# A row sum over 64 MB: groups of 16 rows on one load queue, VectorE for the bulk, and a last group in falling pieces

## The chip, the cores and the metric

The kernel runs on one core of one Trainium2 chip. The metric is the device time of one execution in microseconds (us). All times below are medians of several executions unless a single profiled one is named. A profiled execution has a *span*, from its first to its last instruction; the measured time of the same execution is about 1.8 us longer. Comparisons use runs called fast. On one core, a run is called slow only when it is over 1.5% above the fastest run of the same kernel.

## The reference

```python
batch, seq, dim = 32, 512, 1024
x = np.random.randn(batch, seq, dim).astype(np.float32)      # 67.1 MB

def reference(x):
    return np.sum(x, axis=-1).astype(np.float32)              # 16,384 sums
```

Each of 16,384 rows of 1,024 floats becomes one sum. The kernel reads 67.1 MB and writes 0.07 MB, with one addition per element read.

## The kernel before

Rows are cut into 16 tiles. A tile has 128 partitions with 8 consecutive rows each, 32 KB per partition. Even tiles are summed by one VectorE reduce, odd tiles by 8 ScalarE activations that accumulate. The loads of the even tiles, and of all tiles from 12 on, are issued by SyncE, those of the odd tiles up to 11 by ScalarE, so two queues are in use. The last two tiles are loaded in four pieces of two rows each.

```python
P, Q = 128, 8;  W = Q * dim;  ntiles = 16
head_launchers = [nc.sync, nc.scalar] * 6
# pools: input tiles bufs=5, scratch bufs=4, one tile "stage" for all sums
for i in range(ntiles):
    t = inpool.tile([P, W], fp32)
    eng = head_launchers[i] if i < len(head_launchers) else nc.sync
    dst = stage[:, i * Q : (i + 1) * Q]
    if i >= ntiles - 2:                       # the last two tiles
        engs = ["s","v","s","v"] if i == ntiles - 2 else ["v","v","v","v"]
        for s in range(4):                    # four loads of 2 rows
            nc.sync.dma_start(out=t[:, s*2*dim : (s+1)*2*dim], in_=...)
        for s in range(4): ...                # "v": one reduce of 2 rows; "s": two activations
    elif i % 2 == 0:
        eng.dma_start(out=t, in_=x_t[i])
        nc.vector.tensor_reduce(out=dst, in_=t.rearrange("p (q d) -> p q d", q=Q),
                                axis=X, op=add)
    else:
        eng.dma_start(out=t, in_=x_t[i])
        for q in range(Q):
            nc.scalar.activation(out=sc, in_=t[:, q*dim:(q+1)*dim], func=Copy,
                                 accum_out=dst[:, q:q+1])
    # after every second tile: store by GpSimd; the last store by SyncE
```

Of the kernel before, what the change touches and what calls it, by code (L numbers as in the profile page):

```python
# [1 line left out]

# [4 lines left out]


@with_exitstack
def kernel(  # L10
    ctx: ExitStack,
    tc: tile.TileContext,
    x: bass.AP,
    out: bass.AP,
):
    nc = tc.nc
    fp32 = mybir.dt.float32

    batch, seq, dim = x.shape
    rows = batch * seq  # L20
    P = 128
    Q = 8
    W = Q * dim
    ntiles = rows // (P * Q)

    x_t = x.flatten_outer_dims().rearrange("(n p q) d -> n p (q d)", p=P, q=Q, n=ntiles)
    out_v = out.rearrange("b s -> (b s)").rearrange("(n p q) -> p n q", p=P, q=Q, n=ntiles)

    bounds = list(range(2, ntiles - 1, 2)) + [ntiles - 1, ntiles]

    head_launchers = [nc.sync, nc.scalar] * 6

    with (
        tc.tile_pool(name="in", bufs=5) as inpool,
        tc.tile_pool(name="scratch", bufs=4) as spool,
        tc.tile_pool(name="stage", bufs=1) as stpool,
    ):
        stage = stpool.tile([P, ntiles * Q], fp32)

        prev = 0  # L40
        for i in range(ntiles):
            t = inpool.tile([P, W], fp32)
            eng = head_launchers[i] if i < len(head_launchers) else nc.sync
            dst = stage[:, i * Q : (i + 1) * Q]
            if i >= ntiles - 2:
                NSUB = 4
                QS = Q // NSUB
                engs = (
                    ["s", "v", "s", "v"] if i == ntiles - 2 else ["v", "v", "v", "v"]
                )  # L50
                for s in range(NSUB):
                    nc.sync.dma_start(
                        out=t[:, s * QS * dim : (s + 1) * QS * dim],
                        in_=x_t[i][:, s * QS * dim : (s + 1) * QS * dim],
                    )
                for s in range(NSUB):
                    sdst = dst[:, s * QS : (s + 1) * QS]
                    if engs[s] == "v":
                        nc.vector.tensor_reduce(  # L59
                            out=sdst,  # L60
                            in_=t[:, s * QS * dim : (s + 1) * QS * dim].rearrange(
                                "p (q d) -> p q d", q=QS
                            ),
                            axis=mybir.AxisListType.X,
                            op=mybir.AluOpType.add,
                        )
                    else:
                        for q in range(s * QS, (s + 1) * QS):
                            sc = spool.tile([P, dim], fp32)
                            nc.scalar.activation(  # L70
                                out=sc,
                                in_=t[:, q * dim : (q + 1) * dim],
                                func=mybir.ActivationFunctionType.Copy,
                                accum_out=dst[:, q : q + 1],
                            )
            elif i % 2 == 0:
                eng.dma_start(out=t, in_=x_t[i])  # L77
                nc.vector.tensor_reduce(  # L78
                    out=dst,
                    in_=t.rearrange("p (q d) -> p q d", q=Q),  # L80
                    axis=mybir.AxisListType.X,
                    op=mybir.AluOpType.add,
                )
            else:
                eng.dma_start(out=t, in_=x_t[i])  # L85
                for q in range(Q):
                    sc = spool.tile([P, dim], fp32)
                    nc.scalar.activation(  # L88
                        out=sc,
                        in_=t[:, q * dim : (q + 1) * dim],  # L90
                        func=mybir.ActivationFunctionType.Copy,
                        accum_out=dst[:, q : q + 1],
                    )
            if (i + 1) in bounds:
                n0, n1 = prev, i + 1
                prev = i + 1
                src = stage[:, n0 * Q : n1 * Q].rearrange("p (n q) -> p n q", q=Q)
                oeng = nc.sync if n1 == ntiles else nc.gpsimd
                oeng.dma_start(out=out_v[:, n0:n1], in_=src)  # L99


# [1 line left out]
_INS = ['x']  # L103
_OUTS = [((32, 512), 'float32')]


# [23 lines left out]
```

## Time and profile before

| | before |
|---|---|
| time, median (range) | 165.8 us (165.76 to 165.94) |
| span of the profiled run | 164.1 us |
| VectorE busy, ScalarE busy | 74.5 us, 64.3 us |
| share of loads in the chain of waits | 86% |

From the page of the profile: the busy time of each engine, the chain that ended last by engine, and the two groups of VectorE reduces (line, engine, operation, tiles, shapes, count, then busy time and mean ns of one, then idle time before them and what ended it).

```profile
DVE 74.5 (45%) x13; ACT 64.3 (39%) x121; POOL 5.9 (4%) x12
...
DMA 86%; DVE 7%; ACT 5%; issue 0%; ACTq 0%; SPq 0%
...
L78 DVE TENSOR_REDUCE stage<-t 128x8 f32<-128x8192 f32 x7 | 60.8, 8686 | 71.6 <-DMA t<-in_x_dram 71.6
L59 DVE TENSOR_REDUCE stage<-t 128x2 f32<-128x2048 f32 x6 | 13.7, 2286 | 15.6 <-DMA t<-in_x_dram 15.6
```

Both engines that add (DVE is VectorE, ACT is ScalarE) are idle more than half the time, and what ends their idle time is a load (apart from 1.7 us of ScalarE at the start). So the loads set the kernel's time. A row costs VectorE (8,686 - 2,286) / 6 = 1,067 ns, and a reduce has about 150 ns on top.

The end of the chain of waits of the kernel before, in order of time (start us, us, what):

```profile
99.84 39.72 DMA t<-in_x_dram
139.55 0.02 issue
139.57 19.87 DMA t<-in_x_dram
159.44 0.02 issue
159.47 2.29 DVE stage L59
```

Tile 13 landed at 139.55 us and the last piece at 159.44 us. Then one reduce of two rows takes 2.29 us, and the final store and the end of the program take the other 2.3 us of the span. There are two places to gain: the loads, and the 4.7 us after the last load.

### The profile page before, as it was taken

The numbers are of one execution on the slowest core, as the hardware profiler recorded it, in microseconds if no ns is written. First come the engines' busy times: TensorE is split into PE (matmuls) and PEld (weight loads), VectorE is DVE, ScalarE is ACT, GpSimd is POOL, SyncE is SP. The second block draws the span as 40 slices with busy tenths as digits, with TensorE's granted clock in tenths as the row PEclk, the third lists the DMA queues.
The fourth block names the chain that finished last, engine by engine and source line by source line (L and its number), as shares of the span: only waits on it lengthen the run. The fifth ranks groups of instructions, "written<-read, shape, count | busy, mean of one in ns | idle before, by whom it ended". The sixth has DMA issues, their size and how long they took to land.

```text
span 164.1 us, 241 instructions
## 1 busy us (share of the span) xinstructions
DVE 74.5 (45%) x13; ACT 64.3 (39%) x121; POOL 5.9 (4%) x12
## 2 busy tenths in 40 slices
DVE  0000049600794990039700892595008920055994
ACT  3000049600693000099101980000496006999940
POOL 0000000200001000000100001000001000010110
DMA  7899999998999989999999899999999998999960
GB/s 256 383 479 415 407 479 391 447 449 383 503 391 439 457 384 471 423 407 479 391 441 455 385 471 415 409 479 399 439 447 391 472 417 383 421 423 419 423 243 1
DMA packets 3569, 67.18 MB, mean 409 GB/s; under 512 B 640, under 2 KB 752, under 8 KB 752
## 3 DMA queue, kind: packets, MB, share of 16 engines
q1 hardware_dynamic: 2448, 41.95, 60.1%
q10 hardware_dynamic: 864, 25.17, 35.5%
q0 software_dynamic: 256, 0.06, 0.2%
q14 instruction: 1, 0.01, 0.0%
HBM read 67.11 MB, written 0.07 MB: 409 GB/s over the span
## 4 chain that ended last, share of the span: by engine, by line
DMA 86%; DVE 7%; ACT 5%; issue 0%; ACTq 0%; SPq 0%
DMA t<-in_x_dram 86%; DVE stage L78 5%; ACT sc L88 5%; DVE stage L59 1%; ACTq L85 0%; SPq L77 0%; SPq L85 0%; ACTq L88 0%
## 5 line engine op out<-in xcount | busy, mean ns | idle before, releaser
L88 ACT ACTIVATE sc<-t 128x1024 f32<-128x1024 f32 x56 | 58.3, 1041 | 91.7 <-DMA t<-in_x_dram 91.7
L78 DVE TENSOR_REDUCE stage<-t 128x8 f32<-128x8192 f32 x7 | 60.8, 8686 | 71.6 <-DMA t<-in_x_dram 71.6
L59 DVE TENSOR_REDUCE stage<-t 128x2 f32<-128x2048 f32 x6 | 13.7, 2286 | 15.6 <-DMA t<-in_x_dram 15.6
L99 POOL DMA_DIRECT2D out_dram<-stage x8 | 5.7, 718 | 152.3 <-ACT sc L88 98.8
L88 ACT ACTIVATION_READ_ACCUMULATOR sc<-t 128x1 f32 x56 | 10.4, 186 | 0.0
L70 ACT ACTIVATE sc<-t 128x1024 f32<-128x1024 f32 x4 | 4.2, 1039 | 0.0
L88 ACT ACT_TABLE_LOAD x1 | 1.3, 1283 | 1.7 <-PEq L114 1.7
L70 ACT ACTIVATION_READ_ACCUMULATOR sc<-t 128x1 f32 x4 | 0.7, 185 | 0.0
L114 POOL MEMSET const-float32-0.0<- 128x1 f32 x1 | 0.1, 99 | 0.2 <-issue 0.2
L114 POOL MEMSET const-bfloat16-1.0<- 128x1 bf16 x1 | 0.1, 102 | 0.0
L114 POOL MEMSET const-float32-1.0<- 128x1 f32 x1 | 0.1, 99 | 0.0
L114 POOL MEMSET const-uint8-127<- 128x1 uint8 x1 | 0.1, 99 | 0.0
## 6 DMA issues: line engine op xcount, KB each, us to landing
t<-in_x_dram SPq DMA_DIRECT2D x8, 4096.0 KB, 39.8
t<-in_x_dram ACTq DMA_DIRECT2D x6, 4096.0 KB, 31.0
t<-in_x_dram SPq DMA_DIRECT2D x8, 1024.0 KB, 27.5
out_dram<-stage POOLq DMA_DIRECT2D x7, 8.0 KB, 8.0
out_dram<-stage POOLq DMA_DIRECT2D x1, 4.0 KB, 1.7
out_dram<-stage SPq DMA_DIRECT2D x1, 4.0 KB, 1.4
```

The source lines that it names most:

```text
L59: nc.vector.tensor_reduce(out=sdst, in_=t[:, s * QS * dim : (s + 1) * QS * dim].rearrange("p (q d) -> p q d", q=QS), axis=mybir.AxisListTy ...
L70: nc.scalar.activation(out=sc, in_=t[:, q * dim : (q + 1) * dim], func=mybir.ActivationFunctionType.Copy, accum_out=dst[:, q : q + 1],)
L78: nc.vector.tensor_reduce(out=dst, in_=t.rearrange("p (q d) -> p q d", q=Q), axis=mybir.AxisListType.X, op=mybir.AluOpType.add,)
L88: nc.scalar.activation(out=sc, in_=t[:, q * dim : (q + 1) * dim], func=mybir.ActivationFunctionType.Copy, accum_out=dst[:, q : q + 1],)
L99: oeng.dma_start(out=out_v[:, n0:n1], in_=src)
L114: nc = _bacc.Bacc("TRN2", target_bir_lowering=False, num_devices=1)
```

## The change

The intent: larger loads (16 rows, 64 KB per partition), all issued by SyncE; VectorE alone sums six of the seven large groups, and the two engines share the seventh; the eighth group comes in pieces of 8, 4, 2 and 1 rows, and its very last row in 384, 384 and 256 columns, so that little is left to add after the last landing; the sums of the first groups are stored by GpSimd while loads still run. The diff, cut to its core:

```diff
-    Q = 8
-    x_t = x.flatten_outer_dims().rearrange("(n p q) d -> n p (q d)", p=P, q=Q, n=ntiles)
-    head_launchers = [nc.sync, nc.scalar] * 6
-        tc.tile_pool(name="in", bufs=5)  ...  scratch bufs=4
+    BIG = 16
+    x_g = x.flatten_outer_dims().rearrange("(g p j) d -> g p j d", p=P, j=BIG)
+    nbig = J // BIG - 1                       # 7
+    tail = [(8, 4), (4, 2), (2, 1)]           # (rows, of them ScalarE's)
+        tc.tile_pool(name="in", bufs=3)  ...  scratch bufs=1
...
+        def rows_of(t, a, n, j, n_act):
+            nv = n - n_act
+            block = t[:, a * dim : (a + n) * dim].rearrange("p (n d) -> p n d", d=dim)
+            nc.sync.dma_start(out=block, in_=rows_from(j, n))
+            if nv:
+                vec(sums[:, j : j + nv], block[:, :nv, :])
+            for q in range(nv, n):
+                act(sums[:, j + q : j + q + 1], block[:, q, :], dim)
...
+        for i in range(nbig):
+            t = inpool.tile([P, BIG * dim + 2], fp32)
+            rows_of(t, 0, BIG, i * BIG, BIG // 2 if i == nbig - 1 else 0)
+            if i % 3 == 2:
+                store(nc.gpsimd, i - 2, i + 1)
+        store(nc.gpsimd, nbig - 1, nbig)
+        t = inpool.tile([P, BIG * dim + 2], fp32)
+        for n, n_act in tail:
+            rows_of(t, a, n, nbig * BIG + a, n_act);  a += n
+        rows_of(t, a, 1, nbig * BIG + a, 1);  a += 1
+        last = t[:, a * dim :]
+        cuts = [0, 384, 768, dim]
+        for c0, c1 in zip(cuts, cuts[1:]):
+            nc.sync.dma_start(out=last[:, c0:c1], in_=rows_from(j, 1)[:, 0, c0:c1])
+        # partial sums of columns 0-383 and 384-767 go to the two cells behind the row,
+        # so the last reduce adds 256 columns and the two partial sums: 258 elements
+        store(nc.sync, nbig, nbig + 1)
```

In what follows, a *descriptor* is one contiguous piece of a load, here one partition's rows, moved by one of the 16 DMA engines. The traces show it as a packet: each load has 128, 8 per engine.

More of the change, by code (lines that the diff above doesn't have):

```diff
@@ L17 @@
     fp32 = mybir.dt.float32
+    P = 128
     batch, seq, dim = x.shape
     rows = batch * seq
-    P = 128
-    Q = 8
-    W = Q * dim
-    ntiles = rows // (P * Q)
-    x_t = x.flatten_outer_dims().rearrange("(n p q) d -> n p (q d)", p=P, q=Q, n=ntiles)
-    out_v = out.rearrange("b s -> (b s)").rearrange("(n p q) -> p n q", p=P, q=Q, n=ntiles)
-    bounds = list(range(2, ntiles - 1, 2)) + [ntiles - 1, ntiles]
-    head_launchers = [nc.sync, nc.scalar] * 6
+    J = rows // P
+    BIG = 16
+    x_g = x.flatten_outer_dims().rearrange("(g p j) d -> g p j d", p=P, j=BIG)
@@ L33, with rows_from @@
+    out_v = out.rearrange("b s -> (b s)").rearrange("(g p j) -> p g j", p=P, j=BIG)
+    def rows_from(j, n):
+        return x_g[j // BIG, :, j % BIG : j % BIG + n, :]
+    nbig = J // BIG - 1
+    tail = [(8, 4), (4, 2), (2, 1)]
     with (
-        tc.tile_pool(name="in", bufs=5) as inpool,
-        tc.tile_pool(name="scratch", bufs=4) as spool,
+        tc.tile_pool(name="in", bufs=3) as inpool,
+        tc.tile_pool(name="scratch", bufs=1) as spool,
         tc.tile_pool(name="stage", bufs=1) as stpool,
@@ L37 @@
     ):
-        stage = stpool.tile([P, ntiles * Q], fp32)
-        prev = 0
-        for i in range(ntiles):
-            t = inpool.tile([P, W], fp32)
-            eng = head_launchers[i] if i < len(head_launchers) else nc.sync
-            dst = stage[:, i * Q : (i + 1) * Q]
-            if i >= ntiles - 2:
-                NSUB = 4
-                QS = Q // NSUB
-                engs = (
-                    ["s", "v", "s", "v"] if i == ntiles - 2 else ["v", "v", "v", "v"]
-                )
-                for s in range(NSUB):
-                    nc.sync.dma_start(
-                        out=t[:, s * QS * dim : (s + 1) * QS * dim],
-                        in_=x_t[i][:, s * QS * dim : (s + 1) * QS * dim],
-                    )
-                for s in range(NSUB):
-                    sdst = dst[:, s * QS : (s + 1) * QS]
-                    if engs[s] == "v":
-                        nc.vector.tensor_reduce(
-                            out=sdst,
-                            in_=t[:, s * QS * dim : (s + 1) * QS * dim].rearrange(
-                                "p (q d) -> p q d", q=QS
-                            ),
-                            axis=mybir.AxisListType.X,
-                            op=mybir.AluOpType.add,
-                        )
-                    else:
-                        for q in range(s * QS, (s + 1) * QS):
-                            sc = spool.tile([P, dim], fp32)
-                            nc.scalar.activation(
-                                out=sc,
-                                in_=t[:, q * dim : (q + 1) * dim],
-                                func=mybir.ActivationFunctionType.Copy,
-                                accum_out=dst[:, q : q + 1],
-                            )
-            elif i % 2 == 0:
-                eng.dma_start(out=t, in_=x_t[i])
-                nc.vector.tensor_reduce(
-                    out=dst,
-                    in_=t.rearrange("p (q d) -> p q d", q=Q),
-                    axis=mybir.AxisListType.X,
-                    op=mybir.AluOpType.add,
-                )
-            else:
-                eng.dma_start(out=t, in_=x_t[i])
-                for q in range(Q):
-                    sc = spool.tile([P, dim], fp32)
-                    nc.scalar.activation(
-                        out=sc,
-                        in_=t[:, q * dim : (q + 1) * dim],
-                        func=mybir.ActivationFunctionType.Copy,
-                        accum_out=dst[:, q : q + 1],
-                    )
-            if (i + 1) in bounds:
-                n0, n1 = prev, i + 1
-                prev = i + 1
-                src = stage[:, n0 * Q : n1 * Q].rearrange("p (n q) -> p n q", q=Q)
-                oeng = nc.sync if n1 == ntiles else nc.gpsimd
-                oeng.dma_start(out=out_v[:, n0:n1], in_=src)
@@ new lines, with vec, act @@
+        sums = stpool.tile([P, J], fp32)
+        scratch = spool.tile([P, dim], fp32)
+        def vec(dst, src):
+            nc.vector.tensor_reduce(
+                out=dst, in_=src, axis=mybir.AxisListType.X, op=mybir.AluOpType.add
+            )
+        def act(dst, src, n):
+            nc.scalar.activation(
+                out=scratch[:, :n],
+                in_=src,
+                func=mybir.ActivationFunctionType.Copy,
+                accum_out=dst,
+            )
+        def rows_of(t, a, n, j, n_act):
[6 more added lines that the diff above has]
+                act(sums[:, j + q : j + q + 1], block[:, q, :], dim)
@@ new lines, in store @@
+        def store(eng, g0, g1):
+            eng.dma_start(
+                out=out_v[:, g0:g1],
+                in_=sums[:, g0 * BIG : g1 * BIG].rearrange("p (g j) -> p g j", j=BIG),
+            )
+        for i in range(nbig):
[5 more added lines that the diff above has]
+        t = inpool.tile([P, BIG * dim + 2], fp32)
@@ new lines @@
+        a = 0
+        for n, n_act in tail:
+            rows_of(t, a, n, nbig * BIG + a, n_act)
+            a += n
+        rows_of(t, a, 1, nbig * BIG + a, 1)
+        a += 1
+        j = nbig * BIG + a
+        last = t[:, a * dim :]
+        cuts = [0, 384, 768, dim]
+        for c0, c1 in zip(cuts, cuts[1:]):
+            nc.sync.dma_start(out=last[:, c0:c1], in_=rows_from(j, 1)[:, 0, c0:c1])
+        for i, (c0, c1) in enumerate(zip(cuts, cuts[1:])):
+            if c1 < dim:
+                vec(last[:, dim + i : dim + i + 1], last[:, c0:c1])
+            else:
+                vec(sums[:, j : j + 1], last[:, c0 : dim + i])
```

## The prediction

> **What bounds the kernel now.** The loads. In the chain of waits the loads hold 86% of the 164.1 us span; VectorE is busy 45% and ScalarE 39% (busy table). Tiles 0 and 1 land at 22.6 us and tile 13 at 139.55 us (idle before the first reduces, and the chain): 50.3 MB in 117 us, 430 GB/s. The last two tiles, cut into 8 KB rows per partition, land from 139.55 to 159.44 us: 8.39 MB at 422 GB/s. After the last landing come one 2,286 ns VectorE reduce (2 rows), a 0.35 us issue, and about 2 us of store and end; the unprofiled time is 1.7 us over the span.
>
> **What the change does, costed.**
>
> 1. Bulk work moves from half VectorE, half ScalarE to VectorE alone. The 8-row reduce takes 8,686 ns, the 2-row one 2,286 ns: about 1,067 ns a row and 150 ns fixed. A 16-row group then costs about 17.2 us (estimate) against 19.5 us between group landings. VectorE keeps pace; with three buffers, load k+3 is issued about 2 us before load k+1 lands, with load k+2 queued. So the move is off the critical path, gain zero.
>
> 2. Descriptor size. From the two rates, one engine takes about 1,218 ns for 32 KB and 311 ns for 8 KB: about 8 ns fixed plus 27.1 B/ns (estimate; the Trainium skill, "DMA: Bandwidth & Descriptors", section "Where 436 GB/s comes from", gives a fabric ceiling of 435 GB/s). Descriptors per engine fall from 176 to 112: about 0.5 us. If the 16 rows stayed 4 KB descriptors, the fit gives 411 GB/s, a loss of several us.
>
> 3. One queue instead of two: nothing. The skill (same page, "Issuing engines are not separate DMA queues") says that issuing from several engines saves only sequencer time; an issue here takes 0.33 us.
>
> 4. The end. The last piece is 256 columns. Its reduce over 258 elements is estimated at 0.42 us, against 2.29 us now. Pieces arrive about 0.3 to 0.45 us apart, and the two 384-column reduces (about 0.55 us each) lag slightly, so VectorE ends some 0.7 us after the last landing: about 1.6 us gained. ScalarE's last row (1.04 + 0.19 us) lands 1.2 us before the end and just fits. The final store stays.
>
> 5. Fewer GpSimd stores (8 become 3): these queues moved 0.06 MB, 0.2% of the DMA; gain 0.1 us or none.
>
> **Sum.** 165.8 - 1.6 (end) - 0.5 (descriptors) = 163.7 us; 8 in 10 between 162.8 and 164.8. Faster by over 2% (under 162.5): 0.07; within 2%: 0.90; slower by over 2%: 0.03.
>
> **What would show it.** Group landings about 19.5 us apart, about 431 GB/s between them. VectorE about 75% busy, idle before each group's reduce for about 2 us. Load packets fall as counted. The last load lands at about 158.9 us. After it VectorE works 0.6 to 0.8 us, and the chain ends with that, the SyncE store and about 2 us.
>
> **What would make it wrong.** Rows not merged into one descriptor (slower, 168 to 170). A slower read pattern from the 64 KB spacing of partitions. Late issue of load k+3, if the wait for VectorE leaves too little queued. Small transfers at the end completing later than their bytes explain; or ScalarE's last row or a GpSimd store ending last. On the good side: costs of descriptors or of two queues greater than fitted.

## The result, and the profile after

The changed kernel takes 163.84 us (163.67 to 164.03) against 165.8 us. The ratio is 0.9879, with a 95% interval of 0.9865 to 0.9893. A ratio here is the mean time of one kernel's fast runs over that of the other's in the same rounds, so it is not quite the ratio of the medians. The gain of 2.0 us is clear of the noise.

From the page of the profile after: busy times, the load queue (packets, MB, share of 16 engines), the chain by engine, and the issue of the very last piece (KB, us to landing).

```profile
DVE 121.4 (75%) x13; ACT 19.7 (12%) x33; POOL 2.4 (1%) x7
...
q1 hardware_dynamic: 2160, 67.12, 96.6%
...
DMA 74%; DVE 22%; SPq 1%; issue 0%; DVEq 0%
...
t<-in_x_dram SPq DMA_DIRECT2D x1, 128.0 KB, 38.4
```

The timeline of VectorE after (start us, us, engine, line, operation, tiles, count; in brackets the idle time before it and what ended it; the line at 153.70 merges a two-row and a one-row reduce):

```profile
22.78 17.22 DVE L44 TENSOR_REDUCE sums<-t 128x16 f32<-128x16384 f32 x1 [22.78 <-DMA t<-in_x_dram]
42.11 17.22 DVE L44 TENSOR_REDUCE sums<-t 128x16 f32<-128x16384 f32 x1 [2.11 <-DMA t<-in_x_dram]
...
138.94 8.69 DVE L44 TENSOR_REDUCE sums<-t 128x8 f32<-128x8192 f32 x1 [2.15 <-DMA t<-in_x_dram]
148.68 4.42 DVE L44 TENSOR_REDUCE sums<-t 128x4 f32<-128x4096 f32 x1 [1.05 <-DMA t<-in_x_dram]
153.70 3.62 DVE L44 TENSOR_REDUCE sums<-t 128x2 f32<-128x2048 f32 x2 [0.59 <-DMA t<-in_x_dram]
158.00 1.01 DVE L44 TENSOR_REDUCE t<-t 128x1 f32<-128x384 f32 x2 [0.69 <-DMA t<-in_x_dram]
159.05 0.42 DVE L44 TENSOR_REDUCE sums<-t 128x1 f32<-128x258 f32 x1
```

Each large reduce starts when its group lands, after 2.1 us of waiting: VectorE has 2.1 us to spare per group. From the first landing to the seventh (22.78 to 138.94) six groups take 116.16 us; the kernel before needed 116.95 us for the same bytes (22.6 to 139.55). The changed kernel's second profile, of the next section, has 116.43 us, so such a figure moves by 0.3 us from run to run. The last piece lands at about 158.7 us: it was issued at 120.3 us and took 38.4 us. VectorE ends at 159.47 us, 0.8 us later, where it was 2.3 us before. So the last landing moved forward by some 0.7 us in this pair of profiles, and the time after it shrank by 1.5 us.

### The profile page after: what moved, and what is told of

Its sections match the earlier page's. It is cut to its first block, busy times and chain, and to the rows that moved or that the text cites. A ratio compares the mean times of both kernels' runs of the same rounds, so it can differ in the third digit from the quotient of the medians.

```text
span 161.9 us, 124 instructions
## 1 busy us (share of the span) xinstructions
DVE 121.4 (75%) x13; ACT 19.7 (12%) x33; POOL 2.4 (1%) x7
## 3 DMA queue, kind: packets, MB, share of 16 engines
q1 hardware_dynamic: 2160, 67.12, 96.6%
## 4 chain that ended last, share of the span: by engine, by line
DMA 74%; DVE 22%; SPq 1%; issue 0%; DVEq 0%
DMA t<-in_x_dram 74%; DVE sums L44 22%; SPq L59 1%; DVE t L44 1%; DVEq L44 0%
## 5 line engine op out<-in xcount | busy, mean ns | idle before, releaser
L44 DVE TENSOR_REDUCE sums<-t 128x16 f32<-128x16384 f32 (+5 forms) x11 | 120.4, 10941 | 37.4 <-DMA t<-in_x_dram 37.3
L49 ACT ACTIVATE scratch<-t 128x1024 f32<-128x1024 f32 x16 | 16.9, 1057 | 138.2 <-DMA t<-in_x_dram 137.8
L66 POOL DMA_DIRECT2D out_dram<-sums x3 | 2.2, 733 | 146.6 <-DVE sums L44 135.8
L49 ACT ACTIVATION_READ_ACCUMULATOR scratch<-t 128x1 f32 x16 | 3.0, 186 | 0.0
L44 DVE TENSOR_REDUCE t<-t 128x1 f32<-128x384 f32 x2 | 1.0, 546 | 0.7 <-DMA t<-in_x_dram 0.7
## 6 DMA issues: line engine op xcount, KB each, us to landing
t<-in_x_dram SPq DMA_DIRECT2D x1, 128.0 KB, 38.4
```

What stands on the lines that cost most here:

```text
L44: nc.vector.tensor_reduce(out=dst, in_=src, axis=mybir.AxisListType.X, op=mybir.AluOpType.add)
L49: nc.scalar.activation(out=scratch[:, :n], in_=src, func=mybir.ActivationFunctionType.Copy, accum_out=dst,)
L66: eng.dma_start(out=out_v[:, g0:g1], in_=sums[:, g0 * BIG : g1 * BIG].rearrange("p (g j) -> p g j", j=BIG),)
```

## The experiments

Twelve runs were made, one of them the changed kernel again. Their diffs are cut to the core too, with comments in place of some code. Each call also ran the kernel before on the same chip (medians 165.82 to 165.88 us), and the first of the three calls ran the changed kernel again, as a partner for the others.

> The changed kernel once more, as the partner on this chip for the other three. Both theories: 163.8 us, ratio 0.988 to the kernel before, groups landing 19.36 us apart.

Measured: 163.86 us (163.75 to 163.99), ratio 0.9882. The result repeats.

### Which half gives what: the two ends and the two ways of loading

First the changed kernel with the end of the kernel before:

```diff
-        for n, n_act in tail: rows_of(t, a, n, ...)
-        ... one row, then 384, 384, 256 columns
+        for a in range(0, BIG, 2):
+            rows_of(t, a, 2, nbig * BIG + a, 2 if a in (0, 4) else 0)
```

> The changed kernel with the end of the kernel before: the last 16 rows in eight pieces of two rows, the last four on VectorE. My theory: 1.5 us slower than the changed kernel, 165.3 us, so the loads alone gave 0.4 to 0.5 us. Rival (the bulk gave most): under 0.9 us slower, 164.7 or less.

Measured: 165.33 us, ratio 0.997 (0.9958 to 0.9982). The end is worth 1.5 us on the changed kernel, as expected; the rest of the change is worth 0.5 us.

Then the opposite: the kernel before, of which only the last tile gets falling pieces, all on VectorE.

```diff
+            if i == ntiles - 1:
+                # loads: rows 0-1, 2-3, 4-5, 6, then row 7 in columns 0-383, 384-767, 768-1023
+                # sums: all by VectorE, as in the changed kernel
```

> The kernel before with only its last 8-row tile changed: pieces of 2, 2, 2, 1 rows and of 384, 384 and 256 columns, all on VectorE. My theory: the end alone gives 1.4 to 1.6 us of the 1.9, so 164.3 us; VectorE ends 0.6 to 0.9 us after the last landing instead of 2.3. Rival (most of the gain is from the bulk's loads): under 0.9 us, 164.9 or more.

Measured: 166.03 us, ratio 1.0009 (0.9997 to 1.0022). Nothing was gained. This was a miss, and a useful one. The timeline of VectorE at the end of this kernel, each line from a window around it (the first line merges a two-row and a one-row reduce):

```profile
154.41 2.29 DVE L49 TENSOR_REDUCE stage<-t 128x2 f32<-128x2048 f32 x1 [0.19 <-DMA t<-in_x_dram]
156.91 3.41 DVE L49 TENSOR_REDUCE stage<-t 128x2 f32<-128x2048 f32 x2 [0.22 <-DMA t<-in_x_dram]
160.24 1.00 DVE L49 TENSOR_REDUCE t<-t 128x1 f32<-128x384 f32 x2
161.28 0.42 DVE L49 TENSOR_REDUCE stage<-t 128x1 f32<-128x258 f32 x1
```

The last three lines have no wait for a load. From 156.91 us on, VectorE works without a pause until 161.70 us, and all loads had landed at about 159.6 us (the last was issued at 147.0 and took 12.6). A pair of rows takes VectorE 2.29 us and arrives every 2.49 us, so VectorE is only just ahead, and each further piece adds its fixed cost. Two rows cut into four pieces cost 1.21 + 0.54 + 0.54 + 0.42 = 2.7 us where one reduce took 2.29. These small pieces alone don't shorten the end; the reading to test next is that VectorE must also have less to do there.

So the next kernel took over the whole end: tiles 13 and 14 half on each engine, tile 15 in pieces of 4, 2 and 1 rows shared by both engines, then the three column pieces.

```diff
+            if i >= ntiles - 3:
+                if i < ntiles - 1:
+                    piece(0, Q, Q // 2)          # 4 rows VectorE, 4 rows ScalarE
+                else:
+                    piece(0, 4, 2); piece(4, 2, 1); piece(6, 1, 1)
+                    # row 7 in 384, 384 and 256 columns on VectorE
```

> The kernel before with the whole end of the changed one: tiles 13 and 14 half on each engine, tile 15 in pieces of 4, 2 and 1 rows shared by VectorE and ScalarE, then the last row in 384, 384 and 256 columns. Theory (falling pieces pay only when both engines share them, since a row takes VectorE 1.07 us and arrives every 1.24, and each piece adds a fixed cost): VectorE is done 0.6 to 0.9 us after the last landing, 164.3 us. Rival (the end pays nothing on the 8-row kernel, the gain is tied to the large groups): 165.7 or more.

Measured: 164.12 us (164.06 to 164.25), ratio 0.9898 (0.9884 to 0.9911). Its VectorE at the end:

```profile
156.43 1.22 DVE L49 TENSOR_REDUCE stage<-t 128x1 f32<-128x1024 f32 x1 [0.24 <-DMA t<-in_x_dram]
158.35 1.01 DVE L49 TENSOR_REDUCE t<-t 128x1 f32<-128x384 f32 x2 [0.70 <-DMA t<-in_x_dram]
159.39 0.42 DVE L49 TENSOR_REDUCE stage<-t 128x1 f32<-128x258 f32 x1
```

VectorE waits for the last row again (0.70 us) and is done at 159.81 us. Two more things differ from the kernel that gained nothing: the pieces are of 4, 2 and 1 rows instead of 2, 2, 2 and 1, and tile 14 comes in one load. They were not tested apart from the sharing; the wait of 0.70 us, where the other kernel had none, is what speaks for the sharing. That closes the square (us; the kernel before stayed between 165.82 and 165.88):

| | old end | new end |
|---|---|---|
| loads of the kernel before | 165.8 | 164.12 |
| loads of the changed kernel | 165.33 | 163.86 |

The new end gives 1.5 to 1.7 us. The new loads, with whatever one queue, fewer stores and the move to VectorE add, give 0.3 to 0.5 us. The end explains most of the result, and it doesn't need large groups.

### The size of a load's rows

The changed kernel with each large group loaded by two transfers of 8 rows (32 KB per partition):

```diff
-            nc.sync.dma_start(out=block, in_=rows_from(j, n))
+            step = 8 if n == BIG else n
+            for r in range(0, n, step):
+                nc.sync.dma_start(out=block[:, r:r+step, :], in_=rows_from(j + r, step))
```

> The changed kernel with each 16-row group loaded by two transfers of 32 KB per partition; same buffers, reduces, queue and stores. Theory A (each descriptor has a fixed cost of about 8 ns on its engine): 56 more descriptors per engine, 0.45 us slower than the changed kernel, 164.3 us, groups 19.43 us apart. Theory B (the gain between landings comes from one queue or fewer stores): no change, 163.8 us and 19.36 us.

Measured: 164.04 us (164.00 to 164.69) against 163.86 (163.75 to 163.99) for the changed kernel on the same chip. The medians differ by about 0.2 us rather than 0.45. The four runs of each just don't overlap, but the intervals of the two ratios do (0.9877 to 0.9907, and 0.9868 to 0.9895), and two of the four runs of the changed kernel in the result above (163.96 and 164.03 us) lie about as high, so a difference is not shown beyond the noise. The landings can't settle it: from the second to the sixth the steps average 19.47 us here and 19.41 in the changed kernel's profile, but other profiles with 64 KB rows have from 19.37 (the changed kernel's first) to 19.47 (a kernel below with half of the bulk on ScalarE). (The first step took 20.01 us; this profile is of the slowest run of that kernel, and I can't say why.) The direction is that of theory A; the size is open.

To see the fixed cost well above the noise, the next kernel spaces the rows by 1,026 elements in the buffer, so that a row can't join the next and goes as a 4 KB descriptor of its own. Transfers, bytes and sums are the same.

```diff
+            pitch = dim + 2 if n == BIG else dim
-            block = t[:, a * dim : (a + n) * dim].rearrange("p (n d) -> p n d", d=dim)
+            block = t[:, a*pitch : (a+n)*pitch].rearrange("p (n d) -> p n d", d=pitch)[:, :, :dim]
```

> The changed kernel with rows spaced by 1026 elements in the buffer, so that the bulk goes as 4 KB descriptors, 16 times as many, in the same transfers. Fixed cost of 8 ns per descriptor: groups land 20.4 us apart instead of 19.36 (411 GB/s), 170.6 us. If the size of a descriptor did not matter: 163.8 us.

Measured: 171.58 us (171.55 to 171.62), ratio 1.0344. The load queue's line and two landings, read from VectorE's timeline:

```profile
q1 hardware_dynamic: 15600, 67.12, 98.4%
...
24.09 17.22 DVE L44 TENSOR_REDUCE sums<-t 128x16 f32<-128x16384 f32 x1 [24.09 <-DMA t<-in_x_dram]
...
146.87 8.69 DVE L44 TENSOR_REDUCE sums<-t 128x8 f32<-128x8192 f32 x1 [3.26 <-DMA t<-in_x_dram]
```

The packets grew from 2,160 to 15,600. Six groups take 122.78 us, 20.46 us each (20.4 expected) or 410 GB/s, against 19.36 us and 433 GB/s. The 1.10 us per group over 120 more descriptors per engine is 9.2 ns each (the spacing also moves the rows off multiples of 4 KB in the buffer, and what that costs was not tested). The total is 1 us above the expectation; the first group alone lands 1.4 us later, of which 1.1 is the step itself. The records of single packets in the changed kernel's trace, whose last group comes in pieces of falling size, say nearly the same. Their median times:

| packet | 4 KB | 8 KB | 16 KB | 32 KB | 64 KB |
|---|---|---|---|---|---|
| ns on one engine | 159 | 309 | 611 | 1213 | 2418 |

From 4 to 64 KB the time grows by 2,259 ns for 61,440 bytes, 27.2 bytes per ns, and the line leaves 8.4 ns at zero bytes. (The 4 KB packets of the spaced rows have a median of 164 ns instead of 159.) With 16 engines the slope is 435 GB/s, the ceiling that the Trainium skill gives ("DMA: Bandwidth & Descriptors", "Where 436 GB/s comes from"). The changed kernel's bulk runs at 433 GB/s, so the bulk of the loads has almost nothing left to give.

### One queue, and VectorE alone

The prediction gave both of these zero. Four kernels test them. First the kernel before with all loads on SyncE's queue:

```diff
-    head_launchers = [nc.sync, nc.scalar] * 6
+    head_launchers = [nc.sync]
```

> The kernel before with all loads on the SyncE queue. Theory A (queues matter for the order of landing only, and two engines with five buffers keep up with either order): 165.8 us within 0.2. Theory B (taking turns between queues costs the DMA engines time, the part of the 0.8 us between landings that descriptors leave over): 165.3 us.

Measured: 166.01 us (165.87 to 166.06), ratio 1.0009 (0.9997 to 1.0022). There is no gain, so two queues don't slow the DMA engines, as theory A has it.

Now the changed kernel with the odd groups loaded from ScalarE's queue:

```diff
-            nc.sync.dma_start(out=block, in_=rows_from(j, n))
+            ldeng = nc.scalar if (n == BIG and (j // BIG) % 2) else nc.sync
+            ldeng.dma_start(out=block, in_=rows_from(j, n))
```

> The changed kernel with the odd 16-row groups loaded from the ScalarE queue, the rest from the SyncE queue. Theory A: nothing, 163.8 us within 0.2. Theory B (two queues taking turns on one DMA engine cost something): 0.3 to 0.8 us slower.

Measured: 171.83, 170.66, 167.64, 170.69 and 167.45 us. Three of the five are called slow, because they lie over 1.5% above the fastest; the two fast ones give a ratio of 1.0104. Every run is at least 3.4 us above any run of the changed kernel. Neither theory had this. The profile is of the slowest run (170.1 us span), so only the order of landing and VectorE's work are used from it; the start at 42 us comes back below in a kernel with fast runs alone. VectorE's timeline and the totals of the waits:

```profile
42.20 68.60 DVE L44 TENSOR_REDUCE sums<-t 128x16 f32<-128x16384 f32 x4 [42.20 <-DMA t<-in_x_dram]
110.97 17.22 DVE L44 TENSOR_REDUCE sums<-t 128x16 f32<-128x16384 f32 x1 [0.17 <-DMA t<-in_x_dram]
132.81 33.46 DVE L44 TENSOR_REDUCE sums<-t 128x16 f32<-128x16384 f32 x5 [4.62 <-DMA t<-in_x_dram]
...
SPq L60 <- DVE sums L44: 72.9, 3, 34.2
```

With two queues the first two groups share the DMA engines (the packet records show one round of 16 packets from one queue, then one from the other) and land together at 42.2 us; with one, group 0 lands at 22.8. VectorE loses its first 19.4 us. It has 120.6 us of work (busy table of this run), and 42.2 + 120.6 is 162.8 us before any further wait, already past the 159.5 us at which the changed kernel is done. With the 2.4 us that follow VectorE's end in both profiles and the 1.8 us between span and measured time this makes 167.0 us, close to the two fast runs (167.64 and 167.45). The profiled slow run has 4.8 us of further waits for loads (0.17 and 4.62), and 171.8 us; why the runs differ in this is open. VectorE runs its first four reduces without a pause, and the load queue waits for it to free buffers (the last line: 72.9 us in three waits). The kernel has become bound by VectorE.

If that is the reason, giving VectorE less work must cure it. The next two kernels give half of every group to ScalarE, with loads issued ahead of the sums (otherwise ScalarE's own load would stand behind its sums):

```diff
+        blocks = [load(k) for k in range(3)]        # two queues: odd k on nc.scalar
         for i in range(nbig):
-            rows_of(t, 0, BIG, i * BIG, BIG // 2 if i == nbig - 1 else 0)
+            vec(sums[:, j : j + 8], block[:, :8, :])
+            for q in range(8, 16): act(sums[:, j + q : j + q + 1], block[:, q, :], dim)
+            if i + 3 < nbig: blocks.append(load(i + 3))
```

> The changed kernel with odd groups on the ScalarE queue and half of every group summed by ScalarE, loads issued ahead of the sums. Theory (two queues hurt the changed kernel because groups 0 and 1 land together at 42 us and VectorE, with only 2.1 us to spare per group, can't catch up): with 8.7 us of VectorE per group it does catch up, and the time returns to 163.8 to 164.3 us although groups 0 and 1 still land together near 42. Rival (two queues slow the loads themselves): 167 us or more, as with VectorE alone.

Measured: 164.39 us (164.15 to 164.65), ratio 0.9913 (0.99 to 0.9927). The loads still come in the same bad order, as VectorE's timeline shows:

```profile
41.95 17.28 DVE L44 TENSOR_REDUCE sums<-t 128x8 f32<-128x8192 f32 x2 [41.95 <-DMA t<-in_x_dram]
68.57 8.69 DVE L44 TENSOR_REDUCE sums<-t 128x8 f32<-128x8192 f32 x1 [9.34 <-DMA t<-in_x_dram]
```

Groups 0 and 1 land together at 41.95 us, and after two reduces VectorE is waiting for loads again. The loss is gone but for half a microsecond (0.4 us against its twin on one queue, the next kernel); the time is 0.1 us over the expected range.

> The same as the last one, but all loads on the SyncE queue: half of every group on ScalarE. Theory (the move of the bulk to VectorE alone is off the critical path with one queue): 163.8 us within 0.2. Rival (VectorE alone issues loads late and costs something): 0.3 us faster or more.

Measured: 164.03 us (163.84 to 164.45), ratio 0.9897. With one queue, sharing the bulk gains nothing over VectorE alone. Moving the bulk to VectorE costs nothing, as long as the loads come one after the other.

### How near the edge the buffers are

```diff
-        tc.tile_pool(name="in", bufs=3) as inpool
+        tc.tile_pool(name="in", bufs=2) as inpool
```

> The changed kernel with two group buffers instead of three. The first load took 22.04 us from issue to landing, 2.7 us more than the 19.36 between landings, and a 17.22 us reduce stands before each issue: a load that finds the queue empty lands 39.6 us after the one two before it, not 38.7. So 0.4 us per group lost, 2.6 us in all, 166.4 us, and the DMA shows gaps. If the order of waits does not matter: 163.8 us.

Measured: 171.89 us (170.66 to 172.49), ratio 1.035. The direction is right, the size is not: 8 us lost rather than 2.6. VectorE's timeline of this kernel:

```profile
22.40 17.22 DVE L44 TENSOR_REDUCE sums<-t 128x16 f32<-128x16384 f32 x1 [22.40 <-DMA t<-in_x_dram]
41.73 17.22 DVE L44 TENSOR_REDUCE sums<-t 128x16 f32<-128x16384 f32 x1 [2.11 <-DMA t<-in_x_dram]
63.75 17.22 DVE L44 TENSOR_REDUCE sums<-t 128x16 f32<-128x16384 f32 x1 [4.80 <-DMA t<-in_x_dram]
83.29 17.22 DVE L44 TENSOR_REDUCE sums<-t 128x16 f32<-128x16384 f32 x1 [2.32 <-DMA t<-in_x_dram]
105.45 17.22 DVE L44 TENSOR_REDUCE sums<-t 128x16 f32<-128x16384 f32 x1 [4.94 <-DMA t<-in_x_dram]
```

Two of these steps are 22 us instead of 19.4. The next two, to 125.19 and 144.72 us, are 19.7 and 19.5, and then the first piece of the last group lands 12.4 us later, instead of 9.9 in the changed kernel. These three delays make 7.8 of the 8 us.

The third load was issued at 39.65 us, when its buffer came free, 2.1 us before the second landed, and it took 24.1 us to land, 2.4 us longer than the first (0.74 to 22.40). My estimate took the first load's time as that of any load on an empty queue; a queue that is just running dry costs more than that. The packet records show where: the engines were done with the second load between 40.89 and 41.37 us, but their first packets of the third began between 41.14 and 43.58 us, the first of them 1.5 us after the issue, and a packet of this load took 2.53 us on average where one of the second took 2.42 (0.9 us over the 8 packets of an engine). Why they begin so unevenly and run slower at first is left open. The three late loads were issued 2.1 to 2.3 us before the landing ahead of them; the one issued 2.5 us before (at 122.69) lost only 0.1 us, so the edge lay near 2.4 us in this trace. Three buffers hide all of it, because a whole load is always queued behind the one in flight.

### The early stores

The changed kernel with no early stores, one store of all sums at the end:

```diff
-            if i % 3 == 2: store(nc.gpsimd, i - 2, i + 1)
-        store(nc.gpsimd, nbig - 1, nbig)
-        store(nc.sync, nbig, nbig + 1)
+        store(nc.sync, 0, nbig + 1)
```

> The changed kernel with no early stores: one store of all 64 KB at the end by SyncE. Theory A (early stores cost the loads nothing and hide their own time): the end grows by the longer store, 0.3 to 1 us slower, landings unchanged at 19.36 us. Theory B (stores disturb the load stream): landings closer together by 0.05 us or more, and no slower overall.

Measured: 164.24 us (164.14 to 164.79), ratio 0.9906 (0.9893 to 0.9918) against 0.9882 for the changed kernel in another call: about 0.4 us slower. The issue table, with the changed kernel's final store in the first fence and this kernel's in the second (KB, us to landing):

```profile
out_dram<-sums SPq DMA_DIRECT2D x1, 8.0 KB, 1.4
```

```profile
out_dram<-sums SPq DMA_DIRECT2D x1, 64.0 KB, 2.2
```

The final store is 0.8 us longer, and the landings stay 19.37 us apart on average (22.53 to 138.74 us over six groups, against 19.36 and 19.41 in the two profiles of the changed kernel). Early stores cost the loads nothing that can be seen here, and they hide most of 0.8 us. Both kernels of the comparison have early stores, so this is no part of the 2.0 us.

## Why the prediction was right

The predicted 163.7 us was measured as 163.84. Point by point:

- **The loads bound the kernel, and the bulk's move to VectorE is free.** This held. VectorE is busy 75% (75% predicted) and waits 2.1 us before each large reduce (about 2 predicted); sharing the bulk with ScalarE (164.03 us) is not faster. The Trainium skill ("VectorE: DVE Perf Modes", "The perf-mode tier table") gives this reduce only the slowest mode, 1x, and its "Specifications" a clock of 0.96 GHz; 1,024 elements at one per cycle would be an estimated 1,067 ns, and the trace has (17,219 - 8,686) / 8 = 1,067 ns a row.
- **Descriptors, 0.5 us.** The mechanism held. The fixed cost, fitted from two rates before the change as 8 ns, is 8.4 ns in the packet records and 9.2 ns in the 4 KB experiment. The yield was less sure: each of three comparisons takes away 56 descriptors per engine (0.5 us by the packet records), and they gave 0.5 and 0.3 us in the square and 0.2 us with the large groups in 32 KB rows, the last not clear of the noise.
- **The end, 1.6 us.** It measured 1.5 and 1.7 us in the two rows of the square. VectorE ended 0.8 us after the last landing, at the upper edge of the predicted 0.6 to 0.8, and ScalarE's last row fitted (it ended at 158.6 us). But the prediction's reason, that the last reduce is short, is only half of it. The same three column pieces, after pieces of 2, 2, 2 and 1 rows and all on VectorE, gain nothing (166.03 us). They pay when ScalarE takes half of the rows before them, so that VectorE waits for the last row and not the row for VectorE. The prediction has ScalarE's share of the end in it ("just fits"), but not that the gain hangs on it.
- **One queue, "nothing".** This is right for the kernel before (166.01 us on one queue) and wrong as a statement about the change. In the changed kernel the single queue is a condition: with two, every run lost at least 3.4 us (fast runs 167.45 and 167.64 us), as VectorE, alone with the bulk, started 19 us late and could not catch up. The argument counted bytes per second and forgot the order of landing.
- **Fewer stores, 0.1 us or none.** Removing all early stores left the landings where they were; no gain from fewer could be seen.

No experiment points to a version that beats the changed kernel. Its bulk runs within 0.5% of the slope of its packets, and 0.8 us lies between the last landing and the end of the sums.

## What to carry to other kernels

When a kernel is bound by its loads, the work left after the last landing is where time is to be had. Cut it into falling pieces, but first see whether the engine that takes them is idle when they arrive; if it is not, share the rows before them with another engine.

Count the order in which loads land, not only their rate. Two queues move the same bytes per second and deliver the first tile nearly twice as late (42.2 us against 22.8 in the changed kernel, 22.6 against 13.1 in the kernel before), which an engine with 2.1 us to spare per tile can't make good.

Keep one whole load queued behind the one in flight; two buffers instead of three cost 8 us here.

## What the Trainium skill lacked or had wrong

- "DMA: Bandwidth & Descriptors", "Issuing engines are not separate DMA queues", says that issuing on several engines only saves sequencer time. For bandwidth this agrees (166.01 us on one queue, 165.82 on two). It lacks that the interleaving delays the first load: at 42.2 us with two queues against 22.8 with one, which made the changed kernel about 2% slower than itself with one queue (fast runs 167.45 and 167.64 us against 163.86).
- The same page, "Measured", stops at whole transfers issued by GpSimd. A stream from SyncE with 4 KB rows stands only under "iDMA fabric", at 408.7 GB/s, and 410 GB/s agrees with it. What the page lacks is how the time of a descriptor grows with its size for large rows. Measured here: 8.4 ns per descriptor beside 27.2 bytes per ns, with rows from 4 to 64 KB; from 64 to 4 KB per descriptor the stream falls from 433 to 410 GB/s.
- "Where 436 GB/s comes from", on the same page, says that for loads from HBM a limit of about 358 GB/s binds. The condition, both cores of a pair streaming, stands only in the note under "Measured" on that page. With one core running, this case has 433 GB/s in the bulk; the limit did not bind here, as the note has it.
- No page has the cost of letting the load queue run nearly dry. With two buffers, a load issued 2.1 us before the previous one landed took 24.1 us from its issue and landed 22.0 us after that one, against 19.4 us per load in a full queue and 21.7 us from issue to landing for the first load of the same run.
